# Attention heads of a hybrid SSD/MLA step: maxima turned in the next head's first step, rows moved inside SBUF, more remainders and splits on GpSimd, sample queries prepared for two heads at once

## The chip, the cores and the metric

The kernel runs on one core of one Trainium2 chip. The metric is the device time of the whole program in microseconds (us). Before the change the median of three runs is 2051.01 us (2038.73 to 2052.41). The engines are TensorE (PE, with its weight loads PEld), VectorE (DVE), ScalarE (ACT), GpSimd (POOL) and SyncE (SP), which issues DMAs.

## The reference

Two layers, a Mamba-2 SSD layer and a multi-head latent attention (MLA) layer, on a prompt of 1024 tokens and on eight sample sequences of eight tokens with a paged cache of 2048 positions. The change lies in the MLA layer:

```python
def latent_partial(q_lat, q_pe, ckv, kpe, mask):
    s = (jnp.einsum('bqhc,bkc->bhqk', q_lat, ckv.astype(F32))
         + jnp.einsum('bqhr,bkr->bhqk', q_pe.astype(F32), kpe.astype(F32))) * MLA_SCALE
    if mask is not None:
        s = jnp.where(mask, s, NEG_INF)
    m = jnp.max(s, axis=-1)
    p = jnp.exp(s - m[..., None])
    return m, jnp.sum(p, axis=-1), jnp.einsum('bhqk,bkc->bhqc', p, ckv.astype(F32))

def latent_out(l, acc, w_uv):
    return jnp.einsum('bhqc,chv->bqhv', acc / l[..., None], w_uv.astype(F32))
```

16 heads, 64 + 32 query columns (without and with rotary position) a head, 256 latent columns, 64 value columns. The prompt part is causal; `absorb` multiplies the 64 columns of a query by `w_uk` of its head.

## The kernel before

The program has these stages, one behind the other on PE: the SSD layer (to some 1080 us), the MLA input projections and gates, the queries with the first maxima, the sixteen prompt heads (1384 to 1772 us), and the sample attention with the output projection. float32 precision is kept by splitting each operand into a rounded high part and a low part (`split`: a cast on ACT, a subtraction on the engine named, DVE without a name) and adding three matmuls.

`mla_heads` runs the heads in a loop. A head h has 12 steps: for query half qc = 0 four key blocks jb, for qc = 1 eight. A step is `qk` (three matmuls into a PSUM tile `st`, one mask matmul; ACT makes `th`, the rounded exponential, and `P`, the full one; the remainder `tl` = P - th is a subtraction on one engine), then some "units" of preparation, then `pv` of the step two earlier (`LEAD` = 2; matmuls with th and V high, th and V low, tl and V high). So what a step's remainder is needed for comes two steps later. The last `pv` of a query half is followed by the normalisation: ACT (`rl`), DVE and POOL (`og`), a DMA.

The units are generators that run a piece at a time. `maxpass(h + 1, 0)` and `maxpass(h + 1, 1)` (a and b in the loop) compute the scores of the next head once (`sc`), take their row maxima on DVE (`mx`, `tensor_tensor_reduce` and `reduce_max`), turn them to negative split rows (`nm`), transpose these on PE (`nmp`), copy the result (`nr`) on DVE and write it as rows 96 and 97 of the query tile qTh; `qk` of the next head multiplies 98 rows, so that the maximum is subtracted there. `prep(h + 2)` makes the queries of the head after next (`qT`), its part of the sample queries (`qs`, `ql`, `qpr`), keys (`kp`) for every second head, and, for every fourth head, weights and values of a group of four heads (`prep_group`: `w` splits, `vp`). `merge` interleaves the two lists and each step takes its share of them. Odd heads thus have a short list, heads 4, 8 and 12 one with keys, heads 2, 6 and 10 the longest one.

Order: PE and POOL run their instructions in the order in which the program issues them. For DVE, ACT and SP a scheduler decides ahead of the run; each engine then runs its queue in that order. Scores, transposes and preparation share four PSUM buffers (`wt()`).

Lines that matter below: `sc` L1682, `mx` L1685 and L1687, `nm` L1693 and L1694, `nmp` L1697, `nr` L1699, DMAs L1701 and L1702, `st` L1714 to L1721, `th` and `P` L1725 and L1726, `tl` L1728, `pv` L1745 to L1747, `og` L1757 and L1759, `split` L130 and L131, the generic three-matmul product L89 (of `vp` too), `qs` L1645 and L1647, `ql` L1656, `qpr` L1665 to L1667.

Of the kernel before, what the change touches and what calls it, by code (L numbers as in the profile page):

```python
# [20 lines left out]
NT = 8  # L21
# [1472 lines left out]
class Heads:  # L1494
    def __init__(self, k, st):
        tc, nc, I = k.tc, k.nc, k.I
        self.k, self.psum = k, None
        self.wuk = I["mla_w_uk"][0].rearrange("c h n -> c (h n)")
        self.wuv = I["mla_w_uv"][0].rearrange("c h n -> c (h n)")
        vp = st.enter_context(open_pool(tc, name="vp3", bufs=1))  # L1500
        self.V = []
        self.add_v(vp, 0)
        self.w8 = [vp.tile([128, 2, 256], F32R if i > 1 else F32, name=f"w8{i}") for i in range(8)]
        self.kT = [k.kT]
        self.add_k(vp, 1)
        self.qT = []
        self.add_q(vp, 0)
        self.add_q(vp, 1)

# [58 lines left out]
    def units(self, h):  # L1568
        return 4 + 2 * (h % 2 == 0) + 10 * (h % 4 == 0)

    def prep_group(self, hg):
# [9 lines left out]
        split(k, *self.wk, self.wkr)  # L1581
        split(k, *wv, raw)
# [48 lines left out]
    def prep_q(self, h):  # L1631
# [12 lines left out]
        p = self.wt(f"qs{h}")  # L1644
        nc.tensor.transpose(p[:96, :64], self.qt[:64, 8, 96 * j : 96 * j + 96], k.ident[:64, :64])  # L1645
        for c in range(2):
            nc.tensor.transpose(p[:64, 128 + c * 128 : 256 + c * 128],  # L1647
                                self.wkr[:, c, 64 * (h % 4) : 64 * (h % 4) + 64], k.ident)
        qsn = sp.tile([96, 64], F32, tag="qsn", name=f"qsn{h}", bufs=2)
        nc.vector.tensor_copy(qsn, p[:96, :64])  # L1650
        wt = sp.tile([64, 256], F32, tag="wt", name=f"wt{h}", bufs=2)
        nc.scalar.copy(wt, p[:64, 128:384])
        yield
        pl = self.wt(f"ql{h}p")
        for c in range(2):
            nc.tensor.matmul(pl[:, c * 64 : c * 64 + 64], wt[:, c * 128 : c * 128 + 128], qsn[0:64],  # L1656
                             start=True, stop=True)
        for c in range(2):
            src = pl[:, c * 64 : c * 64 + 64].rearrange("p (b t) -> p b t", t=NT)
            dh = k.qlh[:, c].rearrange("p b (h t) -> p b h t", t=NT)[:, :, h]  # L1660
            dl = k.qll[:, c].rearrange("p b (h t) -> p b h t", t=NT)[:, :, h]
            split(k, dh, dl, src)
        src = qsn[64:96].rearrange("p (b t) -> p b t", t=NT)
        qv = k.qpr.rearrange("p b (h t) -> p b h t", t=NT)[:, :, h]
        nc.vector.tensor_copy(qv[0:32], src)  # L1665
        nc.vector.tensor_copy(qv[32:64], src)
        nc.vector.tensor_tensor(qv[64:96], src, qv[0:32].bitcast(F32), op=ALU.subtract)  # L1667
        yield

    def maxpass(self, h, qc):  # L1670
# [29 lines left out]
        nd = k.dram.tile([2, 512], F32, name=f"nd{h}_{qc}")  # L1700
        nc.sync.dma_start(nd.rearrange("a (i c) -> (a i) c", c=128), nr)  # L1701
        nc.sync.dma_start(qh[96:98, 512 * qc : 512 * qc + 512].bitcast(F32), nd)  # L1702

    def qk(self, h, qc, jb):
# [22 lines left out]
        eng = nc.gpsimd if jb % 2 else nc.vector  # L1727
# [45 lines left out]
def mla_heads(k, hd, sm, early, st):  # L1773
    k.tc.keep_in_program_order(k.nc.scalar.preload_act_table_set("natural_log_exp_and_others"))
    held, late = [], []

    def step(g):
        try:
            next(g)
        except StopIteration:  # L1780
            pass

    for h in range(MH):
# [4 lines left out]
        if h + 1 < MH:  # L1788
            a, b = hd.maxpass(h + 1, 0), hd.maxpass(h + 1, 1)
            units += [a] * 4 + [b, a, b, b, b, a] + [b] * 6  # L1790
# [12 lines left out]
        for t in range(12):  # L1803
            qc, jb = (0, t) if t < 4 else (1, t - 4)
            held.append((h, qc, jb, *hd.qk(h, qc, jb)))
            while done < total * (t + 1) // 12:
                step(units[done])
                done += 1
            if len(held) > LEAD:
                hd.pv(*held.pop(0))  # L1810
# [550 lines left out]
```

## Time and profile before

| | us |
|---|---|
| median of three runs | 2051.01 |
| profiled execution | 2054.24 |
| its span, first to last instruction | 2052.5 |
| mean granted PE clock of the span | 0.968 |
| heads stage, 1384 to 1772 | 388.0 |

In the profile a row of the timeline is start, duration, engine, line, operation, output<-input, and, in brackets, the idle time of the engine just before it and what ended that. In the windows each engine's busy time is followed by its number of instructions; PEclk is the share of the full TensorE clock that was granted. A group of instructions by form gives total busy us, mean ns of one, and idle time before them.

### The profile page before, as it was taken

The numbers are of one execution on the slowest core, as the hardware profiler recorded it, in microseconds if no ns is written. First come the engines' busy times: TensorE is split into PE (matmuls) and PEld (weight loads), VectorE is DVE, ScalarE is ACT, GpSimd is POOL, SyncE is SP. The second block draws the span as 40 slices with busy tenths as digits, with TensorE's granted clock in tenths as the row PEclk, the third lists the DMA queues.
The fourth block names the chain that finished last, engine by engine and source line by source line (L and its number), as shares of the span: only waits on it lengthen the run. The fifth ranks groups of instructions, "written<-read, shape, count | busy, mean of one in ns | idle before, by whom it ended". The sixth has DMA issues, their size and how long they took to land.

```text
span 2052.5 us, 33717 instructions
## 1 busy us (share of the span) xinstructions
PE 1932.4 (94%) x12001; PEld 1765.2 (86%) x12001; DVE 1228.3 (60%) x2652; ACT 1111.3 (54%) x2627; POOL 768.2 (37%) x961
## 2 busy tenths in 40 slices
PE   6989999999999999899999999698999999899998
PEld 5879999999999998677788998697888888778887
DVE  4527675757575666544335134468777778776665
ACT  5446666666666666543325224236666667755552
POOL 1317373636455575331000002004232334755541
PEclk9989999999999999899999999899999999999999
DMA  4113323233332333443546321322111112454451
GB/s 147 41 37 91 91 82 93 87 87 96 89 95 86 90 93 125 163 173 125 182 155 197 144 74 50 102 86 65 44 46 35 49 38 76 150 182 126 148 147 38
DMA packets 186479, 206.56 MB, mean 101 GB/s; under 512 B 23132, under 2 KB 151912, under 8 KB 185928
## 3 DMA queue, kind: packets, MB, share of 16 engines
q1 hardware_dynamic: 181480, 185.40, 29.3%
q0 software_dynamic: 4752, 18.88, 2.8%
q8 instruction: 95, 1.56, 0.3%
q14 instruction: 72, 0.59, 0.1%
q10 hardware_dynamic: 80, 0.13, 0.0%
HBM read 151.05 MB, written 53.28 MB: 100 GB/s over the span
## 4 chain that ended last, share of the span: by engine, by line
PE 71%; DVE 10%; DMA 5%; issue 5%; POOL 4%; ACT 4%; SPq 1%; POOLq 0%; DVEq 0%; ACTq 0%
PE pj L89 21%; PE pj L101 8%; PE pq L101 5%; PE pob L101 4%; PE poa L101 4%; PE py L759 3%; POOL kvl L2009 2%; PE pz L101 1%; PE pk L101 1%; PE p L101 1%; PE sc L1682 1%; PE vp L89 1%; PE st L89 1%; PE st L1714 1%; PE st L1716 1%
## 5 line engine op out<-in xcount | busy, mean ns | idle before, releaser
L89 PE MATMUL pj<-xh,wih 128*128 128x384 f32 (+1 forms) x768 | 254.7, 336 | 8.4 <-ACT xh L236 4.1
L89 PE MATMUL pj<-xl,wih 128*128 128x384 f32 (+1 forms) x768 | 254.1, 331 | 0.0
L89 PE MATMUL pj<-xh,wil 128*128 128x384 f32 (+1 forms) x768 | 252.5, 329 | 0.0
L131 DVE TENSOR_TENSOR wil<-wraw,wih 128x512 fp32r<-128x512 f32 x88 | 70.7, 805 | 160.2 <-ACT wih L130 160.1
L1728 POOL TENSOR_TENSOR tl<-P,th 128x384 fp32r<-128x384 f32 (+1 forms) x96 | 91.3, 952 | 185.6 <-ACT P L1726 142.7
L89 PEld LDWEIGHTS pj<-xh,wih 128*128 128x128 f32 x768 | 145.6, 191 | 10.0 <-ACT xh L236 5.0
L89 PEld LDWEIGHTS pj<-xl,wih 128*128 128x128 f32 x768 | 146.0, 190 | 0.6
L89 PEld LDWEIGHTS pj<-xh,wil 128*128 128x128 f32 x768 | 145.7, 190 | 0.0
L101 PE MATMUL pj<-wih,xh 128*128 128x256 f32 x504 | 143.4, 288 | 0.0
L796 POOL TENSOR_TENSOR y<-y,xD 128x256 f32<-128x256 f32 x64 | 83.9, 1311 | 151.5 <-DVE y L795 141.1
L101 PE MATMUL pj<-wil,xh 128*128 128x256 f32 (+1 forms) x504 | 139.2, 282 | 0.0
L1725 ACT ACTIVATE th<-st 128x512 fp32r<-128x512 f32 x192 | 94.3, 491 | 77.8 <-PE st L1721 59.5
L617 DVE SCALAR_TENSOR_TENSOR acc<-raw,vec,acc 128x1112 f32<-128x1112 f32 x84 | 130.3, 1551 | 0.2
L101 PE MATMUL pj<-wih,xl 128*128 128x256 f32 x448 | 126.6, 283 | 0.0
L131 POOL TENSOR_TENSOR xddl<-xdd,xddh 128x256 fp32r<-128x256 f32 x64 | 64.1, 1001 | 116.7 <-ACT xddh L130 116.7
L2009 POOL TENSOR_TENSOR kvl<-pgr,kvh 128x1024 fp32r<-128x1024 f32 x32 | 78.1, 2439 | 70.1 <-ACT kvh L2008 70.1
L130 ACT CAST Ch<-acc 128x128 fp32r<-128x128 f32 x56 | 16.9, 302 | 155.8 <-PE py L89 155.8
L734 ACT ACTIVATE M<-M,tok 128x128 f32<-128x128 f32 (+1 forms) x288 | 90.5, 388 | 10.4 <-DMA M<-acs_d 10.4
L101 PEld LDWEIGHTS pj<-wih,xh 128*128 128x128 f32 x504 | 96.1, 191 | 0.0
L101 PEld LDWEIGHTS pj<-wil,xh 128*128 128x128 f32 (+1 forms) x504 | 93.1, 185 | 0.6
L1726 ACT ACTIVATE P<-st 128x512 f32<-128x512 f32 x192 | 93.2, 485 | 0.0
L101 PEld LDWEIGHTS pj<-wih,xl 128*128 128x128 f32 x448 | 85.6, 191 | 0.0
(1010 smaller groups left out, 6396.8 us busy)
## 6 DMA issues: line engine op xcount, KB each, us to landing
wraw<-in_ssd_w_in SPq DMA_DIRECT2D x92, 256.0 KB
M<-acs_d SPq DMA_DIRECT2D x64, 256.0 KB
y_d<-xD SPq DMA_DIRECT2D x64, 128.0 KB
s<-in_state_ssm SPq DMA_DIRECT2D x32, 256.0 KB
out_s_ssm<-s SPq DMA_DIRECT2D x32, 256.0 KB
wraw<-in_ssd_w_out SPq DMA_DIRECT2D x16, 512.0 KB
q_d<-qt SPq DMA_DIRECT2D x32, 192.0 KB
qp<-q_d SPq DMA_DIRECT2D x8, 768.0 KB
```

The costliest lines, as they stand in the source:

```text
L89: nc.tensor.matmul(out, a, b, start=(i == 0), stop=(i == n - 1))
L101: nc.tensor.matmul(o, a, b, start=(j == 0), stop=(j == len(ops) - 1))
L131: (eng or nc.vector).tensor_tensor(lo, src, hi.bitcast(F32), op=ALU.subtract)
L617: nc.vector.scalar_tensor_tensor(acc, self.raw[bi][:, j : j + n], k.convw[j][:, blk : blk + 1], acc, op0=ALU.mult, op1=ALU.add)
L734: nc.scalar.activation(M[:m, h, :m], M[:m, h, :m], AF.Relu, bias=c.tk[:, 0, 4 * g + h : 4 * g + h + 1], scale=-1.0)
L759: nc.tensor.matmul(py[:m, h * 64 : h * 64 + 64], c.M[:m, h, :m], c.xdt[:m, h * 64 : h * 64 + 64], start=True, stop=True)
L796: nc.gpsimd.tensor_tensor(y[:m], y[:m], c.xD[:m], op=ALU.add)
L1682: nc.tensor.matmul(ps[:, :n], qh[:96, 128 * i : 128 * i + 128], kh[:96, 512 * c : 512 * c + n], start=True, stop=True)
L1725: nc.scalar.activation(th[:, :n], ps[:, :n], AF.Exp, scale=SCALE)
L1726: nc.scalar.activation(P[:, :n], ps[:, :n], AF.Exp, scale=SCALE)
L1728: eng.tensor_tensor(tl[:, :n], P[:, :n], th[:, :n].bitcast(F32), op=ALU.subtract)
L2009: nc.gpsimd.tensor_tensor(rl, raw, rh.bitcast(F32), op=ALU.subtract)
```

## The change

1. The last step of b (transpose `nmp`, copy `nr`, the row DMAs) leaves the head in which its scores are made. It is carried into the first step of the next head, behind that step's `qk` and units.
2. The copied rows go from `nr` in SBUF directly to the query tile, by two DMAs of 4 x 128 values, instead of one DMA to a buffer in HBM and one back.
3. `tl` is made on POOL for jb = 1, 2, 3, 5, 6, 7 (jb % 4 not 0), 9 of the 12 steps of a head, instead of jb odd, 6 of 12.
4. The subtractions of the weight splits in `prep_group` go from DVE to POOL.
5. The sample queries of two heads are made together, in the odd head's preparation: the two transposed queries stand in a block-diagonal tile `qb` (zeroed once on POOL), so that one 128-column matmul per half does what two did; the rotary part `qpr` is written by POOL. Even heads have two units less.

On PE around the end of a head (the end of head 4; `o` is pv, `st` qk, and the number behind a name is that of its buffer) stood before:

```order
L1682 MATMUL sc_71_17300<-kTh_14729,qTh_15805 128x512
L1745 MATMUL o_1_17211<-th,Vh_15808 128x512
L1746 MATMUL o_1_17211<-th,Vl_15809 128x512
L1747 MATMUL o_1_17211<-tl,Vh_15808 128x512
L1714 MATMUL st_1_7_17309<-qTh_14736,kTh_13521 128x128
L1715 MATMUL st_1_7_17309<-qTl_14737,kTh_13521 128x128
L1716 MATMUL st_1_7_17309<-qTh_14736,kTl_13522 128x128
L1721 MATMUL st_1_7_17309<-mr 128x128
L1656 MATMUL ql6p<-qsn_17279,wt_17281 128x64 x2
L1697 MATMUL nmp_1_17330<-ident,nm_1_17303 8x128
L1745 MATMUL o_1_17211<-th,Vh_15808 128x384
L1746 MATMUL o_1_17211<-th,Vl_15809 128x384
```

In the same place on PE stands now:

```order
L1695 MATMUL sc_71_17252<-kTh_14729,qTh_15790 128x512
L1759 MATMUL o_1_17148<-th,Vh_15793 128x384
L1760 MATMUL o_1_17148<-th,Vl_15794 128x384
L1761 MATMUL o_1_17148<-tl,Vh_15793 128x384
L1728 MATMUL st_0_0_17261<-qTh_15790,kTh_14729 128x512
L1729 MATMUL st_0_0_17261<-qTl_15791,kTh_14729 128x512
L1730 MATMUL st_0_0_17261<-qTh_15790,kTl_14730 128x512
L1735 MATMUL st_0_0_17261<-mr 128x128
L1695 MATMUL sc_00_17273<-kTh_15774,qTh_14733 128x128
L1710 MATMUL nmp_1_17276<-ident,nm_1_17255 8x128
L1759 MATMUL o_1_17148<-th,Vh_15793 128x256
L1760 MATMUL o_1_17148<-th,Vl_15794 128x256
```

The last scores `sc_71` moved a step later, and `nmp` moved behind the first step's qk of the next head; the `ql` matmuls are gone from this even head.

On POOL around the start of a head whose units hold a group's splits (the end of head 5 and the start of head 6; `tl` of 384 columns is the second step's) stood before:

```order
L1728 TENSOR_TENSOR tl<-P,th 128x384
L1728 TENSOR_TENSOR tl<-P,th 128x128
L1728 TENSOR_TENSOR tl<-P,th 128x384
L1759 TENSOR_TENSOR og_17382<-og_17382,rl_1_17383 64x512
L1728 TENSOR_TENSOR tl<-P,th 128x128
L1728 TENSOR_TENSOR tl<-P,th 128x512
L1759 TENSOR_TENSOR og_17472<-og_17472,rl_0_17473 64x512
```

and now:

```order
L1742 TENSOR_TENSOR tl<-P,th 128x384
L1742 TENSOR_TENSOR tl<-P,th 128x256
L1678 CAST qpr<-qsr_17442 32x8x16
L1679 CAST qpr<-qsr_17442 32x8x16
L1680 TENSOR_TENSOR qpr<-qsr_17442,qpr 32x8x16
L1742 TENSOR_TENSOR tl<-P,th 128x128
L1742 TENSOR_TENSOR tl<-P,th 128x384
L131 TENSOR_TENSOR w_14724<-w_14721,w_14723 128x512
L131 TENSOR_TENSOR w_14728<-w_14722,w_14727 128x512
L1773 TENSOR_TENSOR og_17583<-og_17583,rl_1_17584 64x512
L1742 TENSOR_TENSOR tl<-P,th 128x256
L1742 TENSOR_TENSOR tl<-P,th 128x128
```

Between the second step's remainder and `og` two splits came in, the third step's remainder (256 columns) stands behind `og`, and the casts of `qpr` stand before the last remainder of the head ahead.

The diff, cut to its core:

```diff
--- before.py
+++ after.py
@@ -1506,6 +1506,9 @@
         self.qT = []
         self.add_q(vp, 0)
         self.add_q(vp, 1)
+        self.qb = [vp.tile([128, 128], F32, name="qb")]
+        for t in self.qb:
+            nc.gpsimd.memset(t, 0.0)
 
     def start(self, st):
         k, nc = self.k, self.k.nc
@@ -1566,7 +1569,7 @@
         yield from self.prep_q(h)
 
     def units(self, h):
-        return 4 + 2 * (h % 2 == 0) + 10 * (h % 4 == 0)
+        return 4 + 10 * (h % 4 == 0)
 
     def prep_group(self, hg):
         k, nc = self.k, self.k.nc
@@ -1578,8 +1581,8 @@
         raw, wv = w8[1], w8[6:]
         nc.sync.dma_start(raw, self.wuv[:, cs].rearrange("(k p) e -> p k e", p=128))
         yield
-        split(k, *self.wk, self.wkr)
-        split(k, *wv, raw)
+        split(k, *self.wk, self.wkr, nc.gpsimd)
+        split(k, *wv, raw, nc.gpsimd)
         yield
         vh, vl = self.V[hg % 2]
         for i in range(8):
@@ -1641,30 +1644,40 @@
             cs = slice(512 * c, 512 * c + 512)
             split(k, qh[:96, cs], ql[:96, cs], p[:96])
             yield
-        p = self.wt(f"qs{h}")
-        nc.tensor.transpose(p[:96, :64], self.qt[:64, 8, 96 * j : 96 * j + 96], k.ident[:64, :64])
+        if j == 0:
+            return
+        p = self.wt(f"qs{pr}")
+        for jj in range(2):
+            nc.tensor.transpose(p[:96, 64 * jj : 64 * jj + 64], self.qt[:64, 8, 96 * jj : 96 * jj + 96], k.ident[:64, :64])
+        o = (pr % 2) * 128
         for c in range(2):
-            nc.tensor.transpose(p[:64, 128 + c * 128 : 256 + c * 128],
-                                self.wkr[:, c, 64 * (h % 4) : 64 * (h % 4) + 64], k.ident)
-        qsn = sp.tile([96, 64], F32, tag="qsn", name=f"qsn{h}", bufs=2)
-        nc.vector.tensor_copy(qsn, p[:96, :64])
-        wt = sp.tile([64, 256], F32, tag="wt", name=f"wt{h}", bufs=2)
-        nc.scalar.copy(wt, p[:64, 128:384])
+            nc.tensor.transpose(p[:, 128 + c * 128 : 256 + c * 128], self.wkr[:, c, o : o + 128], k.ident)
+        qb = self.qb[0]
+        for jj in range(2):
+            r = slice(64 * jj, 64 * jj + 64)
+            nc.vector.tensor_copy(qb[r, r], p[0:64, r])
+        qr = sp.tile([32, 128], F32, tag="qsr", name=f"qsr{pr}", bufs=1)
+        nc.vector.tensor_copy(qr, p[64:96, :128])
+        wt = sp.tile([128, 256], F32, tag="wt", name=f"wt{pr}", bufs=1)
+        nc.scalar.copy(wt, p[:, 128:384])
         yield
-        pl = self.wt(f"ql{h}p")
+        pl = self.wt(f"ql{pr}p")
         for c in range(2):
-            nc.tensor.matmul(pl[:, c * 64 : c * 64 + 64], wt[:, c * 128 : c * 128 + 128], qsn[0:64],
-                             start=True, stop=True)
+            nc.tensor.matmul(pl[:, c * 128 : c * 128 + 128], wt[:, c * 128 : c * 128 + 128], qb, start=True, stop=True)
+        hs = slice(2 * pr, 2 * pr + 2)
+
+        def pair(t):
+            return t.rearrange("p (j b t) -> p b j t", j=2, t=NT)
+
+        def home(t):
+            return t.rearrange("p b (h t) -> p b h t", t=NT)[:, :, hs]
+
         for c in range(2):
-            src = pl[:, c * 64 : c * 64 + 64].rearrange("p (b t) -> p b t", t=NT)
-            dh = k.qlh[:, c].rearrange("p b (h t) -> p b h t", t=NT)[:, :, h]
-            dl = k.qll[:, c].rearrange("p b (h t) -> p b h t", t=NT)[:, :, h]
-            split(k, dh, dl, src)
-        src = qsn[64:96].rearrange("p (b t) -> p b t", t=NT)
-        qv = k.qpr.rearrange("p b (h t) -> p b h t", t=NT)[:, :, h]
-        nc.vector.tensor_copy(qv[0:32], src)
-        nc.vector.tensor_copy(qv[32:64], src)
-        nc.vector.tensor_tensor(qv[64:96], src, qv[0:32].bitcast(F32), op=ALU.subtract)
+            split(k, home(k.qlh[:, c]), home(k.qll[:, c]), pair(pl[:, c * 128 : c * 128 + 128]))
+        src, qv = pair(qr), home(k.qpr)
+        nc.gpsimd.tensor_copy(qv[0:32], src)
+        nc.gpsimd.tensor_copy(qv[32:64], src)
+        nc.gpsimd.tensor_tensor(qv[64:96], src, qv[0:32].bitcast(F32), op=ALU.subtract)
         yield
 
     def maxpass(self, h, qc):
@@ -1697,9 +1710,10 @@
         nc.tensor.transpose(p[:8, :128], nm.rearrange("p a i -> p (a i)").bitcast(F32), k.ident)
         nr = sp.tile([8, 128], F32, tag="nr", name=f"nr{h}_{qc}", bufs=2)
         nc.vector.tensor_copy(nr, p[:8, :128])
-        nd = k.dram.tile([2, 512], F32, name=f"nd{h}_{qc}")
-        nc.sync.dma_start(nd.rearrange("a (i c) -> (a i) c", c=128), nr)
-        nc.sync.dma_start(qh[96:98, 512 * qc : 512 * qc + 512].bitcast(F32), nd)
+        for a in range(2):
+            row = qh[96 + a : 97 + a, 512 * qc : 512 * qc + 512].bitcast(F32)
+            row = bass.AP(row.tensor, row.offset, [list(row.ap[0]), [128, 4], [1, 128]])
+            nc.sync.dma_start(row, nr[4 * a : 4 * a + 4])
 
     def qk(self, h, qc, jb):
         k, nc, sp = self.k, self.k.nc, self.sp
@@ -1724,7 +1738,7 @@
         P = sp.tile([128, 512], F32, tag="P", name="P", bufs=3)
         nc.scalar.activation(th[:, :n], ps[:, :n], AF.Exp, scale=SCALE)
         nc.scalar.activation(P[:, :n], ps[:, :n], AF.Exp, scale=SCALE)
-        eng = nc.gpsimd if jb % 2 else nc.vector
+        eng = nc.gpsimd if jb % 4 else nc.vector
         eng.tensor_tensor(tl[:, :n], P[:, :n], th[:, :n].bitcast(F32), op=ALU.subtract)
         return th, tl
 
@@ -1772,7 +1786,7 @@
 
 def mla_heads(k, hd, sm, early, st):
     k.tc.keep_in_program_order(k.nc.scalar.preload_act_table_set("natural_log_exp_and_others"))
-    held, late = [], []
+    held, carry = [], None
 
     def step(g):
         try:
@@ -1787,7 +1801,10 @@
             sm.begin(st, hd.psum)
         if h + 1 < MH:
             a, b = hd.maxpass(h + 1, 0), hd.maxpass(h + 1, 1)
-            units += [a] * 4 + [b, a, b, b, b, a] + [b] * 6
+            units += [a] * 4 + [b, a, b, b, b, a] + [b] * 5
+            ready, carry = carry, b
+        else:
+            ready, carry = carry, None
         if h + 2 < MH:
             g = hd.prep(h + 2)
             units = merge(units, [g] * hd.units(h + 2))
@@ -1806,6 +1823,8 @@
             while done < total * (t + 1) // 12:
                 step(units[done])
                 done += 1
+            if t == 0 and ready:
+                step(ready)
             if len(held) > LEAD:
                 hd.pv(*held.pop(0))
     for x in held:
```

## Prediction

> **What bounds the kernel now.** I read the page of the profiled run first, then the windows by stage, the waits of TensorE (PE) in the stage of the sixteen heads, the timeline around one head boundary, and last the groups by form for the price of each operation. The page gives the span and each engine's busy time:
>
> ```profile
> span 2052.5 us, 33717 instructions
> PE 1932.4 (94%) x12001; PEld 1765.2 (86%) x12001; DVE 1228.3 (60%) x2652; ACT 1111.3 (54%) x2627; POOL 768.2 (37%) x961
> ```
>
> PE is busy for 94% of the span, so only time in which PE stands still, or runs at the half clock, or PE work itself, can be won. The edits all lie in the stage of the heads, 1384 to 1772 us. Its windows, with the columns of the first line:
>
> ```profile
> core 0: us, PE busy (x) PEld busy (x) DVE busy (x) ACT busy (x) POOL busy (x), PEclk, DMA share, GB/s
> 1384.00:1772.00 388.00, 364.77 (x1971) 316.12 (x1970) 299.67 (x716) 258.85 (x589) 148.45 (x141) 0.93 0.19 53
> 1500.00:1520.00 20.00, 19.20 (x114) 16.51 (x113) 16.71 (x45) 15.43 (x37) 8.18 (x9) 1.00 0.12 29
> 1520.00:1540.00 20.00, 17.99 (x85) 16.27 (x84) 13.40 (x35) 10.10 (x26) 6.75 (x6) 0.74 0.28 83
> 1600.00:1620.00 20.00, 19.20 (x116) 16.54 (x114) 16.70 (x45) 15.49 (x37) 8.08 (x8) 1.00 0.12 28
> 1620.00:1640.00 20.00, 17.94 (x93) 16.37 (x93) 14.65 (x37) 10.83 (x28) 7.35 (x7) 0.83 0.28 83
> ```
>
> PE idles 388.0 - 364.8 = 23.2 us of this stage. The mean granted clock is 0.93, so 0.07 x 388 = 27 us of full-speed time are not granted either. They come in stretches: 1500 to 1520 has 1.00, the next 20 us 0.74 with fewer matmuls (85 for 114). VectorE (DVE) works 300 of 388 us, GpSimd (POOL) 148. What PE waits for here:
>
> ```profile
> PE nmp L1697 <- DVE nm L1694: 14.0, 11, 2.1
> PE nmp L1697 <- DVE qll L131: 3.2, 4, 0.8
> PE o L1747 <- POOL tl L1728: 0.4, 1, 0.4
> PE o L1747 <- DVE tl L1728: 0.4, 1, 0.4
> ```
>
> 17.2 of the 23.2 us are the transpose nmp, which turns the row maxima of the next head: 15 waits, one at the end of each head but the last. PE takes its instructions in program order, so all of the next head stands behind it. The end of one head in order of time:
>
> ```profile
> 1504.78 0.44 PE L1682 MATMUL sc<-kTh,qTh 96*128 96x512 f32 x1
> ...
> 1505.35 0.76 DVE L1687 CUSTOM_DVE_ANT_0 sc<-sc,mk,mx 128x512 f32<-128x512 f32 x1
> ...
> 1506.25 0.66 PE L1656 MATMUL ql6p<-qsn,wt 64*128 64x64 f32 x4
> ...
> 1506.56 0.42 DVE L1728 TENSOR_TENSOR tl<-P,th 128x256 fp32r<-128x256 f32 x1
> ...
> 1506.88 0.46 POOL L1728 TENSOR_TENSOR tl<-P,th 128x128 fp32r<-128x128 f32 x1 [1.82 <-ACT P L1726]
> 1506.91 0.45 DVE L1693 TENSOR_SCALAR nm<-mx 128x4 fp32r<-128x4 f32 x1
> ...
> 1507.39 0.16 DVE L1694 SCALAR_TENSOR_TENSOR nm<-mx,nm 128x4 fp32r<-128x4 f32 x1
> ...
> 1507.67 0.08 PEld L1697 LDWEIGHTS nmp<-ident,nm 128*8 128x8 f32 x1 [0.91 <-PE ql6p L1656]
> 1507.70 0.27 PE L1697 MATMUL nmp<-ident,nm 128*8 128x128 f32 x1 [0.80 <-DVE qll L131]
> ```
>
> From the last scores (1504.78) to nmp (1507.70) 2.92 us pass. On DVE a remainder of 256 columns stands between the maximum and nm, and nm takes 0.45.
>
> **The change part by part.** *The transpose moves.* Behind the last scores PE will now run three pv matmuls of 384 columns, three of 512, a mask and a narrow score matmul, and only then nmp. Starts of such matmuls in the rows of the next head:
>
> ```profile
> 1513.74 0.34 PE L1747 MATMUL o<-tl,Vh 128*128 128x384 f32 x1
> 1513.91 0.40 PE L1714 MATMUL st<-qTh,kTh 98*128 98x512 f32 x1
> 1514.15 0.40 PE L1715 MATMUL st<-qTl,kTh 98*128 98x512 f32 x1
> ```
>
> 0.17 and 0.24 us apart: 0.24 + 3 x 0.17 + 3 x 0.24, and some 0.1 for the two narrow ones, is 1.6 us from the last scores to nmp. The DVE chain without the remainder and with nm undisturbed is 0.57 to the maximum's start, 0.86 to its end, an estimated 0.17 for nm (about what its second half takes above), and 0.31 from 1507.39 to PE: 1.9 us. Some 0.3 us stay uncovered, 15 times 5 us: the term is -12, between 0 (DVE as late as now) and -17.
>
> *The half clock.* The stretches at the reduced clock begin behind the longer of these waits: in 1500 to 1520 the one wait is the 0.8 above and the clock is full; the row with 0.74 holds this one of 2.0:
>
> ```profile
> 1528.60 0.38 PE L1697 MATMUL nmp<-ident,nm 128*8 128x128 f32 x1 [2.01 <-DVE nm L1694]
> ```
>
>  If such waits shrink, the clock stays up, but new waits (below) can take it down. Of 27 us I take a third, -9, with ends 0 and -20. [...]
>
> *Pairs of sample queries.* The group row of the wide transposes, beside ql6p above:
>
> ```profile
> L1647 PE MATMUL qs<-ident,w 128*64 128x128 f32 x28 | 5.7, 286 | 0.0
> ```
>
> Two heads now use 8 ql matmuls, 2 x 0.66 us; after, 2 wider ones, an estimated 0.4; of six transposes four stay, which spares 2 x 5.7/28 = 0.4 at most. That is about 0.9 us for a pair and seven pairs in this stage: -6, from -3 (latency of a chain counted as work) to -7.
>
> *The rows without the detour through HBM.* Two issues stay two:
>
> ```profile
> 1508.31 0.27 SPq L1701 DMA_DIRECT2D nd<-nr  x1
> 1509.52 0.22 SPq L1702 DMA_DIRECT2D qTh<-nd  x1
> ```
>
> The second now waits for the first to land, 1.2 us from issue to issue. After, both start at once: nr, two issues of 0.27, one landing of up to 1.2. That is some 3 us from nmp. Their reader, the fifth step's qk, stands 4 to 5 us of PE work behind nmp instead of 5.4 to 7.3, because nmp moved towards it. Cost 0 with a spare of about 1 us; if that is gone, see the third rival.
>
> *Remainders and splits to POOL.* Prices by form:
>
> ```profile
> L1728 DVE TENSOR_TENSOR tl<-P,th 128x512 fp32r<-128x512 f32 x64 | 52.4, 818 | 18.0 <-ACT P L1726 17.7
> L1728 POOL TENSOR_TENSOR tl<-P,th 128x512 fp32r<-128x512 f32 x32 | 42.1, 1315 | 44.1 <-ACT P L1726 32.5 <-PE sc L1682 11.0
> L1728 POOL TENSOR_TENSOR tl<-P,th 128x384 fp32r<-128x384 f32 x32 | 34.2, 1069 | 100.5 <-ACT P L1726 82.6 <-PE o L1746 17.8
> L1728 POOL TENSOR_TENSOR tl<-P,th 128x128 fp32r<-128x128 f32 x31 | 14.6, 472 | 38.3 <-ACT P L1726 24.9 <-PE qs L1647 6.7 <-PE nmp L1697 6.4
> L131 DVE TENSOR_TENSOR w<-w,w 128x512 fp32r<-128x512 f32 x5 | 6.5, 1297 | 0.0
> ```
>
> A 256-column remainder on POOL lies between 0.47 and 1.07; I take 0.77. Each head gives POOL one of 512 and two of 256, 1.3 + 2 x 0.77 = 2.9 us, sixteen times 46 us; with six splits of an estimated 1.3 and some 8 for the qpr casts POOL comes to 148 + 62 = 210 of 388 us. In sum it fits; the place is what matters, since POOL is strictly in order. In the head that starts at 1509:
>
> ```profile
> 1511.35 1.02 POOL L1728 TENSOR_TENSOR tl<-P,th 128x384 fp32r<-128x384 f32 x1 [4.02 <-ACT P L1726]
> 1514.32 1.34 POOL L1759 TENSOR_TENSOR og<-og,rl 64x512 f32<-64x512 f32 x1 [1.94 <-PE o L1747]
> 1515.63 0.45 POOL L1728 TENSOR_TENSOR tl<-P,th 128x128 fp32r<-128x128 f32 x1
> ...
> 1515.29 0.28 PE L1747 MATMUL o<-tl,Vh 128*128 128x256 f32 x1
> ```
>
> The third step's remainder (256 columns) is now queued behind og, which ends at 1515.66: it would be ready at 1516.4, and PE asks for it at 1515.29, 1.1 us too early. If DVE, relieved, hands over its part of og sooner, this shrinks. At the seventh step a second og stands in the same way before a remainder of 512. Replaying POOL's queue with the times of before gives 1.1 at the third and 0.55 at the seventh step of the 8 odd heads and 1.3 in three others: 8 x 1.65 + 3.9 = 17 us; 3 if og comes a microsecond sooner. I take +9, the nearer to the row being the upper end, DVE's relief the reason to go below it.
>
> *Splits in the group heads.* In heads 2, 6 and 10 POOL now gets, behind the second step's remainder, two splits, and PE's second vp matmul needs the later one:
>
> ```profile
> 1434.07 0.31 PE L1721 MATMUL st<-mr 128*128 128x128 f32 x1
> ...
> 1435.37 1.00 POOL L1728 TENSOR_TENSOR tl<-P,th 128x384 fp32r<-128x384 f32 x1 [5.43 <-PE o L1746]
> ...
> 1436.21 0.73 PE L89 MATMUL vp<-w,kvh 128*128 128x256 f32 x2
> ```
>
> The remainder ends at 1436.37; two splits of 1.3 end at 1438.97; PE is there at 1436.21 (with the clock halved; a microsecond sooner at the full one). PE waits 2.7 to 3.8 us, three times: +9, from +6 (splits of 0.8, the 512-column row of DVE) to +12. Today DVE makes these splits long before, so nothing of this wait exists. og and the third step's remainder come late behind it, under the same wait.
>
> *The rest.* In the last two heads POOL also makes splits of the gathered cache, and the extra remainders queue with them, each with up to its own 1.3 us: three of them 4, so +2 (0 to 4). The start of the stage and the sample stage keep their order nearly: 0, 3 either way.
>
> **Sum**: -12 - 9 - 6 + 9 + 9 + 2 = -7 us. The profiled execution took 2054.24 us, 1.74 more than its span, and 3.2 more than the median, 2051.01. So 2054.24 - 7 - 3.2 = 2044.
>
> **Rivals.** *First: POOL's lateness is covered.* For it: POOL has 240 us idle here, the relieved DVE brings og forward, and 1 us of lateness is what one matmul group covers. Then nmp's waits and the half clock go: -17 - 20 - 7 + 3 + 6 = -35, 2016 us.
>
> *Second, slower: POOL sets the pace of the pv matmuls.* Place: the remainders behind og and the splits behind the second step's remainder. It decides where a remainder ends on POOL after PE asks for it, which the rows at 1515 already show by 1.1 us. Each such wait takes the place of one at nmp and pulls the clock down again: with +17 for remainders, +12 for splits, +4 at the end, half-clock time up by 7 rather than down, and -5 and -6 for nmp and pairs, +29: 2080 us. Against it: a wait of 0.8 left the clock at 1.00 in the window of 1500.
>
> *Third: the rows come late to the fifth step.* [...] For it: the new transfers are eight pieces of 512 bytes; against it: 1.2 us covered the old one.
>
> *Fourth: the maxima stay as late as they are.* nm took 0.45 beside a POOL remainder of 0.46 that began 0.03 before it, where its second half takes 0.16; a POOL remainder of 512 beside it could hold it 1.3 us, which uses up the ground that nmp gained, and POOL will run more of these. Then nmp keeps its 17 us, the clock wins 4 at most, and POOL's costs come on top: 0 - 4 - 6 + 9 + 9 + 2 = +10, 2061 us. [...]
>
> **How the numbers follow.** About 1% (20.5 us) is what a measurement of this kernel can tell from no change: 2030.5 and 2071.5 are the bounds. Forecast 0.35, first rival 0.33, second 0.18, third 0.07, fourth 0.07. The forecast's own terms reach from -38 to +33; I give 0.02 of it to the faster side. Faster: 0.33 + 0.02 = 0.35; same: 0.33 + 0.07 = 0.40; slower: 0.18 + 0.07 = 0.25. The range takes in the first rival and stops short of the second and third: 2012 to 2075. The forecast's own range, as cases of both signs hold most of the chance, is 2031 to 2064.
>
> **What would show it.** nmp waiting for nm below 6 us in all bears out the first term. PE waiting for POOL's tl by 3 to 17 us, and vp for w by 6 to 12, bear out the costs; if both are near zero, the first rival holds. The clock of the stage tells the second term: 0.95 or more against 0.93. A wait of st for a DMA at the fifth step would be the third rival. What would make me wrong most: a POOL split that runs long before PE asks for it, or waits of 1 us that halve the clock oftener than I took.

## The result and the profile after

The changed kernel takes 2056.99 us (median of 20 runs, 2054.03 to 2059.77), the kernel before 2049.16 us (20 runs, 2038.73 to 2055.07). The ratio is 1.0041, with a 95% interval of 1.003 to 1.0053: the change makes the kernel slower by 0.4%, some 8 us, where a gain of 7 was forecast. The profiled execution of the changed kernel took 2057.51 us, within 1 us of its median; the one of before, 2054.24, lies 5 us above its own.

The page after has less work on PE and DVE, and more on POOL:

```profile
span 2055.7 us, 33651 instructions
...
PE 1917.0 (93%) x11953; PEld 1746.7 (85%) x11953; DVE 1172.9 (57%) x2540; ACT 1108.1 (54%) x2603; POOL 826.8 (40%) x1042
```

PE is busy 15.4 us less (1932.4 before) in a span that is 3.2 us longer: PE stands still for 18.6 us more. The window of the heads stage after, with the columns as in the prediction, and PE's waits in the same window:

```profile
1384.00:1772.00 388.00, 351.38 (x1939) 298.98 (x1938) 250.81 (x619) 256.74 (x570) 204.17 (x216) 0.95 0.20 54
```

```profile
PE o L1761 <- POOL tl L1742: 14.1, 22, 1.1
PE vp L89 <- POOL w L131: 9.6, 3, 3.2
PE o40n L2007 <- ACT pn L2000: 4.4, 1, 4.4
PE nmp L1710 <- DVE nm L1707: 3.5, 6, 0.7
PE o L1761 <- DVE tl L1742: 3.3, 2, 2.8
```

The waits of nmp fell from 17.2 to 3.5 us, as forecast. In their place stand 14.1 us for POOL's remainders (22 waits), 9.6 us for POOL's splits (3 waits), and a wait of 4.4 us in the last head that was 1.2 before. This last one is `o40n`, the first product of the sample attention, whose matmuls already stand between those of head 15; it waits for `pn`, a small copy that ACT makes for it. POOL works 204 us here, close to the 210 that were counted.

Where the time goes by part: the first and the last mask matmul of head 15, after and then before.

```profile
1741.98 0.22 PE L1735 MATMUL st<-mr 128*128 128x128 f32 x1
1771.62 0.27 PE L1735 MATMUL st<-mr 128*128 128x128 f32 x1
```

```profile
1747.83 0.22 PE L1721 MATMUL st<-mr 128*128 128x128 f32 x1
1771.94 0.27 PE L1721 MATMUL st<-mr 128*128 128x128 f32 x1
```

The changed kernel reaches head 15 at 1742.0, 5.8 us ahead, and ends it at 1771.6, 0.3 us ahead: head 15 takes 29.6 us instead of 24.1. What follows takes 2055.7 - 1771.6 = 284.1 us instead of 2052.5 - 1771.9 = 280.6. Against this one execution of before, then, the heads up to 14 did win, and the last head and the sample stage lost it all. Against the second execution of before in the table below, the heads up to 14 do not win: 328.6 us against 325.8. Measured in the same way for every run below, this split (heads 1 to 14; head 15; the rest) carries most of what follows.

### The profile page after: what moved, and what is told of

Read it like the earlier page. It is cut to its first block, busy times and chain, and to the rows that moved or that the text cites. A ratio compares the mean times of both kernels' runs of the same rounds, so it can differ in the third digit from the quotient of the medians.

```text
span 2055.7 us, 33651 instructions
## 1 busy us (share of the span) xinstructions
PE 1917.0 (93%) x11953; PEld 1746.7 (85%) x11953; DVE 1172.9 (57%) x2540; ACT 1108.1 (54%) x2603; POOL 826.8 (40%) x1042
## 4 chain that ended last, share of the span: by engine, by line
PE 70%; DVE 7%; DMA 6%; issue 5%; ACT 5%; POOL 5%; SPq 1%; POOLq 0%; DVEq 0%; ACTq 0%
PE pj L89 21%; PE pj L101 8%; PE pq L101 4%; PE pob L101 4%; PE poa L101 4%; PE py L759 3%; POOL kvl L2028 2%; PE o L1761 1%; PE vp L89 1%; PE pz L101 1%; PE pk L101 1%; DMA tkr<-kpe_dh 1%; PE st L1728 1%; PE p L101 1%; PE st L1729 1%
## 5 line engine op out<-in xcount | busy, mean ns | idle before, releaser
L1742 POOL TENSOR_TENSOR tl<-P,th 128x384 fp32r<-128x384 f32 (+1 forms) x144 | 134.4, 941 | 133.2 <-ACT P L1740 109.7
L130 ACT CAST Ch<-acc 128x128 fp32r<-128x128 f32 x56 | 16.9, 302 | 155.9 <-PE py L89 155.9
L1761 PE MATMUL o<-tl,Vh 128*128 128x512 f32 x192 | 71.4, 372 | 17.4 <-POOL tl L1742 14.1
```

Of the source, the lines that this page charges most:

```text
L1742: eng.tensor_tensor(tl[:, :n], P[:, :n], th[:, :n].bitcast(F32), op=ALU.subtract)
L1761: nc.tensor.matmul(po[:, o:], va, tl[:, :n], start=False, stop=(jb == nj - 1))
```

## The experiments

Each ratio is against the kernel before on the same chip; "heads 1 to 14", "head 15" and "rest" are taken from one profiled execution each, at the mask matmuls as above. Differences between runs are given between medians; reckoned by the ratios they come out up to 3 us otherwise, so a difference of 3 us or less is not told from nothing by the times alone. The parts of one execution differ by chance as well: the same heads 1 to 14 of the changed kernel take 328.6 us here and 326.4, 326.4 and 329.6 in the three runs that edit head 15 only. The windows shown below are all 1402 to 1732 us. This is most of heads 1 to 14; in the faster kernels it reaches into head 15.

| run | median us | ratio, 95% interval | heads 1 to 14 | head 15 | rest |
|---|---|---|---|---|---|
| before (first profile) | 2049.16 | 1 | 336.4 | 24.1 | 280.6 |
| before_again | 2049.06 | 0.9988 [0.9968, 1.0009] | 325.8 | 23.0 | 282.0 |
| the change | 2056.99 | 1.0041 [1.003, 1.0053] | 328.6 | 29.6 | 284.1 |
| splits_on_dve | 2038.43 | 0.9936 [0.9915, 0.9958] | 311.5 | 28.4 | 282.6 |
| remainders_old_rule | 2036.45 | 0.9927 [0.9906, 0.9948] | 313.4 | 23.1 | 282.1 |
| no_pool_moves | 2014.51 | 0.984 [0.9816, 0.9864] | 295.0 | 24.2 | 280.8 |

**The kernel before, a second time** (no edit).

> The kernel before once more, unchanged, for a second profile: its 20 runs spread from 2038.7 to 2055.1 and the profiled one lies at the upper end. Theory (the spread is half-clock time behind the nmp waits, which lie near the length that brings the clock down): a profiled run that is some us faster has fewer half-clock stretches between 1384 and 1772 and the same waits. Rival: the spread comes from another stage (loads from HBM), and the heads stage is equal to 1 us.

The waits of nmp are the same to a tenth of a microsecond, and the clock is not. The windows and the nmp waits in them, the first profile and then the second:

```profile
1402.00:1732.00 330.00, 313.11 (x1704) 272.80 (x1702) 254.03 (x633) 220.39 (x506) 112.50 (x109) 0.92 0.16 46
PE nmp L1697 <- DVE nm L1694: 13.7, 10, 2.1
PE nmp L1697 <- DVE qll L131: 3.2, 4, 0.8
```

```profile
1402.00:1732.00 330.00, 312.04 (x1758) 270.60 (x1756) 262.94 (x653) 227.47 (x520) 119.75 (x116) 0.96 0.19 51
PE nmp L1697 <- DVE nm L1694: 13.7, 10, 2.1
PE nmp L1697 <- DVE qll L131: 3.2, 4, 0.8
```

Both hold 16.9 us of nmp waits (the second has one more wait, of 1.1 us for POOL); 0.92 against 0.96 of the clock is 13 us of full-speed time in 330, and the second execution is 10 us faster, all of it in heads 1 to 14 (325.8 us against 336.4). For this pair the theory holds against the rival: at the same nmp waits the kernel loses 0.04 of its clock more in one execution than in the other. That there is one length near which waits bring the clock down is not shown: in the first profile the waits of 2.04 us that ends at 1431.0 and of 0.85 us that ends at 1461.5 are both followed by a stretch at half the clock, 6.8 and 3.4 us long, and the one of 1.29 us that ends at 1682.3 is not: from 1682 to 1724 the clock is 1.00. The prediction had taken the first execution.

**Splits on DVE again.**

```diff
-        split(k, *self.wk, self.wkr, nc.gpsimd)
-        split(k, *wv, raw, nc.gpsimd)
+        split(k, *self.wk, self.wkr)
+        split(k, *wv, raw)
```

> The changed kernel with the weight splits of a group on DVE again. Theory: the three waits of vp for POOL (9.6 us) and the three half-clock stretches of 6.83 us behind them (10 us of full-speed time) go, heads 2, 6 and 10 shrink from 32.6 to about 27 us, the median falls by 13 to 20 us, to about 2040. Rival (DVE needs the relief): waits of nmp for nm come back at the starts of those heads, 1 to 2 us each with half-clock time, and the median falls by less than 6 us.

2038.43, 18.6 us less than the change. The window and its waits:

```profile
1402.00:1732.00 330.00, 311.11 (x1801) 267.06 (x1801) 230.43 (x578) 236.96 (x525) 173.21 (x187) 1.00 0.19 52
PE o L1761 <- POOL tl L1742: 13.1, 20, 1.1
PE nmp L1710 <- DVE nm L1707: 4.0, 6, 1.0
```

The vp waits are gone, nmp stays at 4 us with the splits on DVE, and the clock is 1.00. So the theory holds and DVE did not need this relief. The row also says something of the second rival: 20 waits of up to 1.1 us for POOL's remainders, and no half clock behind any of them. In the change the same window had three waits of 3.2 us, and 0.97.

**Remainders by the old rule.**

```diff
-        eng = nc.gpsimd if jb % 4 else nc.vector
+        eng = nc.gpsimd if jb % 2 else nc.vector
```

> The changed kernel with the remainders of all heads by the old rule (jb odd on POOL). Theory: the 14.1 us that pv waits for POOL's remainders go, and the nmp waits stay small (under 6 us in all), because the later place of nmp covers DVE's chain without DVE's relief; with the last head's loss gone as well the median falls by 15 to 22 us, to about 2038. Rival (the relief of DVE is what shortened the nmp waits): nmp waits for nm come back to over 10 us, and the median is 2048 or more.

2036.45, 20.5 us less than the change. The window and its waits:

```profile
1402.00:1732.00 330.00, 311.74 (x1786) 271.59 (x1786) 251.69 (x615) 234.76 (x519) 141.19 (x148) 0.96 0.19 51
PE vp L89 <- POOL w L131: 8.9, 3, 3.4
PE nmp L1710 <- DVE nm L1707: 6.7, 6, 1.3
...
PE o L1761 <- POOL tl L1742: 0.6, 1, 0.6
```

POOL's remainders no longer make pv wait; nmp waits 6.7 us, a little over the 6 that the theory gave, far from the rival's 10. Head 15 is back at 23.1 us.

**Both moves to POOL undone**: the two diffs above together; carried transpose, direct rows and pairs stay.

> The changed kernel with both moves to POOL undone: remainders by the old rule and the group's splits on DVE; the carried transpose, the direct rows and the pairs stay. Theory (both moves only cost; their costs add): against the kernel with the old remainder rule (2036.5) the three vp waits (8.9 us) and about 20 us of half clock (10) go as well, the median is 2016 to 2026. Rival (DVE with both loads is too late at the heads' starts): nmp waits come back to over 12 us, the median is 2032 or more.

2014.51, 1.5 us below the expected range. The theory holds: both only cost, and they add. Against this kernel the remainders (splits_on_dve) make heads 1 to 14 longer by 311.47 - 295.03 = 16.4 us and head 15 by 4.2, the splits (remainders_old_rule) heads 1 to 14 by 313.40 - 295.03 = 18.4; the change has 33.6 more there, 5.4 in head 15 and 3.3 behind it. That is 42.3 us, and the medians differ by 42.5. With DVE's remainders and splits as before, its nmp waits are still small:

```profile
1402.00:1732.00 330.00, 320.39 (x1878) 278.88 (x1878) 269.97 (x641) 248.78 (x552) 148.51 (x154) 0.99 0.21 58
PE nmp L1710 <- DVE nm L1707: 4.9, 6, 1.1
```

**The values later, splits on POOL.** This tells the place of a split from its engine.

```diff
     def prep(self, h):
-        yield from self.prep_kv(h)
+        g = self.prep_kv(h)
+        if h and h % 4 == 0:
+            for _ in range(2):
+                next(g)
+                yield
+            yield from self.prep_q(h)
+            yield from g
+            return
+        yield from g
         yield from self.prep_q(h)
```

> The changed kernel, splits still on POOL, but heads 2, 6 and 10 prepare the queries of the head after next before the values: PE comes to the vp matmuls later. Theory (the place in POOL's queue, not the engine's price, makes the three vp waits of 3.2 us, and the half clock is their follower): the vp waits fall from 9.6 us to under 2, the three half-clock stretches go, the median is 2036 to 2044 as with the splits on DVE. Rival (POOL's splits hold up what stands behind them, og and the third step's remainder, whatever PE does): pv waits for POOL instead, in heads 2, 6 and 10, by 2 us or more each, and the median stays over 2048.

2037.66 (0.9952, 0.9934 to 0.997): as much as with the splits on DVE. No wait of vp is left in the window, POOL's remainders are waited for 15.3 us instead of 12.6, and the clock is 0.99:

```profile
1402.00:1732.00 330.00, 310.93 (x1798) 266.92 (x1797) 231.00 (x575) 235.49 (x524) 182.69 (x194) 0.99 0.20 54
PE o L1769 <- POOL tl L1750: 15.3, 23, 1.2
```

The theory holds: the splits cost through the place at which PE asks for them, and not by being on POOL.

**The parts that were meant to win, each alone.** The kernel before with the carried transpose only (parts of the diff of `mla_heads`):

```diff
-            units += [a] * 4 + [b, a, b, b, b, a] + [b] * 6
+            units += [a] * 4 + [b, a, b, b, b, a] + [b] * 5
+            ready, carry = carry, b
...
+            if t == 0 and ready:
+                step(ready)
```

> The kernel before with the carried transpose alone (rows through HBM, queries one head at a time, remainders and splits as before). Theory: the wait of nmp for nm falls from 17.2 to under 8 us without any relief of DVE, and the half-clock stretches of the stage shrink, the median falls from 2050 to 2028 to 2038. Rival (DVE's chain is later than the transpose's new place): nmp waits over 12 us, and the fifth step waits for the rows, which now take two DMAs behind a later start; 2045 or more.

2036.05 (0.9941, 0.9914 to 0.9968): 13 us less than before. DVE's relief is not needed for the nmp waits to go, but the rows through HBM come late in four of the heads, the rival's second half:

```profile
PE st L1714 <- DMA qTh<-nd: 4.6, 4, 2.4
PE nmp L1697 <- DVE nm L1694: 1.8, 4, 0.7
```

The same question in the best kernel, its rows through HBM again (the DMA lines of before put back):

> The kernel with carried transpose, pairs and direct rows (both POOL moves undone), its rows through HBM again. Theory (the carried transpose needs the direct rows, since its rows come 2 to 3 us later: with the transpose alone the fifth step waited 4.6 us for them): waits of st for a DMA of 4 us or more, median 2018 to 2028 against 2014.5. Rival (the rows are hidden either way): no such wait, median 2013 to 2016.

2021.64 (0.9878, 0.9852 to 0.9905), 7.1 us more than no_pool_moves, with 4.1 us of waits of st for the DMA in five steps. The direct rows are worth this, beside a carried transpose.

The kernel before with the pairs of sample queries only (the whole part 5 of the change):

> The kernel before with the sample queries of two heads made together, nothing else. Theory: six us of PE work go (seven pairs of 0.9 us in the heads stage, one before it), and where ql stood between the last scores and nmp its cover goes, so that the nmp waits grow by a few us; net 0 to 6 us below 2050. Rival: the waits take all of it and bring more half clock, 2050 or more.

2021.96 (0.9876, 0.9852 to 0.9899): 27 us where 0 to 6 were expected; neither theory nor rival had it. The nmp waits, with nmp where it was, fell to 9.4 us in 15 waits, none over 1.5, and the clock is whole:

```profile
1402.00:1732.00 330.00, 316.07 (x1847) 273.90 (x1846) 256.69 (x634) 242.59 (x541) 144.57 (x151) 1.00 0.20 55
PE nmp L1710 <- DVE nm L1707: 9.4, 15, 1.5
```

The same with the casts of qpr back on DVE, PE's order unchanged:

```diff
-        nc.gpsimd.tensor_copy(qv[0:32], src)
-        nc.gpsimd.tensor_copy(qv[32:64], src)
-        nc.gpsimd.tensor_tensor(qv[64:96], src, qv[0:32].bitcast(F32), op=ALU.subtract)
+        nc.vector.tensor_copy(qv[0:32], src)
+        nc.vector.tensor_copy(qv[32:64], src)
+        nc.vector.tensor_tensor(qv[64:96], src, qv[0:32].bitcast(F32), op=ALU.subtract)
```

> The kernel with pairs of sample queries alone, its casts of qpr on DVE again; PE's order is the same as with the casts on POOL. Theory (the pairs' 27 us come from PE's work and its order at the end of a head, with DVE's relief a small part): nmp waits 9 to 13 us, the half clock stays away, median 2020 to 2027. Rival (the relief of DVE by the casts is what holds the waits below the length that halves the clock): nmp waits over 14 us, half-clock time over 60 us, median 2035 or more.

2039.96 (0.9961, 0.994 to 0.9981): 18 of the 27 us are gone. The rival holds in the waits (19.0 us, over its 14) and in the time. Its half clock of over 60 us does not show: a clock of 0.98 is some 13 us at half speed in this window.

```profile
1402.00:1732.00 330.00, 308.39 (x1770) 267.21 (x1769) 260.61 (x638) 231.91 (x517) 125.48 (x121) 0.98 0.19 51
PE nmp L1710 <- DVE nm L1707: 19.0, 15, 2.6
```

9.6 us more of waits and 0.02 of the clock in 330 us, 6.6 us, are 16 of the 18. Nearly all of the 9.6 stands at the ends of the seven heads that make the casts, 1.2 to 1.7 us more at each. The timeline shows one group of them:

```profile
1518.44 0.34 DVE L1678 CAST qpr<-qsr 32x128 fp32r<-32x128 f32 x1
1518.79 1.29 POOL L1741 TENSOR_TENSOR tl<-P,th 128x512 fp32r<-128x512 f32 x1
1518.82 1.34 DVE L1679 CAST qpr<-qsr 32x128 fp32r<-32x128 f32 x1
1520.19 0.28 DVE L1680 TENSOR_TENSOR qpr<-qsr,qpr 32x128 fp32r<-32x128 f32 x1
```

The second cast of 32 x 128 takes DVE 1.34 us where POOL has just begun a remainder of 1.29; 1.34 us is also the mean of the seven in the window. The one of the first pair, made at 1349 us, took 0.22. Moved to POOL this cast takes 0.29 to 0.58.

**The last head.** The changed kernel with the old rule for head 15 alone (`jb % (2 if h == MH - 1 else 4)`):

> The changed kernel with one head undone: head 15 makes its remainders by the old rule (jb odd on POOL), all other heads as changed. Theory (the loss sits behind the last head's start: head 15 took 29.6 us against 24.1 before, because extra remainders stand on POOL beside the 2.4 us split of gathered cache rows, a remainder on DVE is held 4.9 us by them, and PE then waits 4.4 us for a copy and runs 10 us at the half clock): the wait of o40n for ACT falls from 4.4 to about 1, head 15 gets 5 us shorter, the median falls from 2057 by 5 to 9 us, to about 2050. Rival (the loss is the sample stage's order alone, or chance of the clock): within 2 us of 2057.

2052.75 (1.0006, 0.9986 to 1.0026): 4.2 us less than the change by the medians, 7 by the ratios, where 5 to 9 were expected; head 15 takes 23.4 us, o40n waits 1.2. The rows of the changed kernel that this undoes, POOL and DVE, then ACT and PE:

```profile
1748.25 1.14 POOL L1742 TENSOR_TENSOR tl<-P,th 128x256 fp32r<-128x256 f32 x2
1749.34 0.60 POOL L1945 CAST tk<-tkr 96x512 fp32r<-96x512 f32 x1
1749.92 2.39 POOL L2028 TENSOR_TENSOR kvl<-pgr,kvh 128x1024 fp32r<-128x1024 f32 x1
1752.28 1.29 POOL L1742 TENSOR_TENSOR tl<-P,th 128x512 fp32r<-128x512 f32 x1
...
1749.22 4.90 DVE L1742 TENSOR_TENSOR tl<-P,th 128x512 fp32r<-128x512 f32 x1 [1.61 <-ACT P L1740]
...
1757.77 0.69 ACT L1971 ACTIVATE P<-sc,nm 128x512 f32<-128x512 f32 x1 [3.68 <-DVE nm L1968]
1759.58 0.24 ACT L2000 COPY pn<-pt40n 8x128 f32<-8x128 f32 x1
1759.87 1.22 PE L2007 MATMUL o40n<-cn,pn 8*128 8x256 f32 x2 [4.39 <-ACT pn L2000]
```

DVE's remainder of 512 columns lasts 4.90 us while POOL works without a gap until 1753.57; nm comes late, and on ACT the small copy pn stands behind the exponential that waits for nm. The scheduler put pn ahead of that exponential before, and again with the old rule in head 15. DVE's remainder, however, stood nearly as long in both: 4.22 us before and 4.20 with the old rule. The rows of before:

```profile
1755.02 4.22 DVE L1728 TENSOR_TENSOR tl<-P,th 128x512 fp32r<-128x512 f32 x1 [1.61 <-ACT P L1726]
1761.49 0.24 ACT L1981 COPY pn<-pt40n 8x128 f32<-8x128 f32 x1
1764.57 0.69 ACT L1952 ACTIVATE P<-sc,nm 128x512 f32<-128x512 f32 x1 [2.84 <-DVE nm L1949]
```

There nm came late too, and cost o40n little (1.2 us), since pn did not stand behind it. So what the change added in head 15 is ACT's order, more than DVE's hold, which grew by 0.7 us only; no run changes the order alone. Two further runs try DVE's remainder alone, by one more `or` in the same line. The first, written with `jb == 4`, moved another key block than the one held:

> The changed kernel with one more remainder on POOL: in head 15 the fifth key block of the second half, the one remainder that DVE held for 4.9 us beside POOL's split of cache rows. [...] Rival (POOL's own lateness is what counts, DVE's long remainder costs nothing): POOL, with 1.3 us more in its queue, makes pv wait longer, and the median is 2057 or above.

2058.21 (1.0054, 1.0032 to 1.0076), where 2050 to 2055 was the author's estimate. The 4.90 us are still there, and so is the wait of 4.4, so it says nothing of what that remainder costs. The second, with `jb == 0`, moves the held one:

> The changed kernel with the remainder of key block 0 of the second half of head 15 on POOL: this is the one that DVE held for 4.9 us (the run last_head_fifth_key_block moved block 4, another one). ACT's order around pn stays as in the changed kernel: pn behind the exponential of the cache scores, which waits for nm from DVE. Theory (two causes in a row: DVE stands while POOL works without a gap, so nm is late, and pn stands behind what waits for nm): nm comes 3 to 4 us sooner, the wait of o40n falls from 4.4 to under 1.5, the median is 2049 to 2055. Rival (DVE waits for POOL or for the scores whatever is taken from it, and only ACT's order counts): o40n still waits 4 us or more, median 2056 or above.

2055.27 (1.0035, 1.0016 to 1.0055), 1.7 us less than the change: in the theory's direction, short of its size (a wait under 1.5, a median to 2055), and too little to tell from nothing by the times. ACT waits 0.96 for nm instead of 3.68, o40n 2.2, head 15 takes 23.8 us. But the next transpose of cache scores, pt, now waits 5.3 us for ACT, and the rest takes 286.9 us instead of 284.1. So within head 15 the loss needs both, pn behind the exponential and a late nm: it goes when either is undone. Most of what this run wins in head 15 is given back in the sample stage.

**A remainder at a better place.** no_pool_moves with one more remainder a head on POOL, key block 6 of the second half, behind no og (`if jb % 2 or jb == 6`):

> The kernel with carried transpose, pairs and direct rows (2014.5), with one more remainder of a head on POOL: key block 6 of the second half, 256 columns, which on DVE stands close ahead of the maxima's end and on POOL behind no og. Theory (what a moved remainder costs is its place: those behind og cost a pv wait of 0.75 to 1.1, this one does not): pv waits for POOL stay under 3 us, the nmp waits fall below 4.9, median 2009 to 2014. Rival (any further POOL work beside DVE's maxima holds up one or the other): pv or nmp waits grow, median 2016 or more.

2013.88, the median of five runs (0.9829, 0.9808 to 0.985), at the upper end of the expected range. nmp waits 3.1 us instead of 4.9, and pv no longer than without this move (1.2 us for DVE and 0.6 for POOL, against 1.3 and 0.7), so a remainder costs nothing that shows at this place; what it wins, 0.6 us between the medians, is too little to tell from nothing. It and no_pool_moves beat both kernels, the one before by 1.6 to 1.7%.

## Why the prediction was wrong, step by step

The step that failed is the price of the moves to POOL, +20 in the sum; they cost 42.5 us. Term by term:

- **The transpose moves, -12**: right. The waits of nmp fell by 13.7 us. The run with this part alone, which relieves DVE of nothing (1.8 us of nmp waits left in the window), shows that the new place did this; the ones with the old remainder rule (6.7) and with both moves undone (4.9) agree.
- **The half clock, -9**: wrong in what it was measured against. The profiled execution of before had 13 us of full-speed time less than its second profile at equal nmp waits. Over the whole stage the clock rose from 0.93 to 0.95, as the prediction asked for; the second profile of before has 0.96 there. And the three vp waits, which the sum counted by their length alone, are each followed by half clock: with the splits on DVE the clock of the window is 1.00, with them on POOL 0.97, 10 us. Around the first of them (1437.3 to 1440.6):

```profile
1420.00:1440.00 20.00, 15.92 (x90) 12.99 (x90) 12.32 (x33) 13.38 (x30) 12.21 (x15) 0.98 0.29 77
1440.00:1460.00 20.00, 19.45 (x105) 17.62 (x106) 9.07 (x23) 10.93 (x25) 8.28 (x9) 0.85 0.15 40
```

  The two rows lack 3.4 us of full-speed time, that is 6.8 us at half the clock, from 1439.2 to 1446.0. The stretches at half the clock last 3.4, 6.8 or 10.2 us in the heads stage of before and 6.8 or 10.2 in that of the change. The length of a wait alone does not decide them: here the clock fell 1.8 us after the wait began, and in the first profile of before three waits of only 0.85 us are each followed by 3.4 us at half the clock (a row of 20 us from 1460 at 0.91), while one of 1.29 us there and 20 of up to 1.1 us in splits_on_dve are followed by none. So the prediction's reading, that the clock falls behind the longer waits alone, was too simple. What decides is not shown here, nor why it differs between executions at equal waits.
- **Pairs, -6**: the sign was right, and a term was missing. Alone they win 27 us, of which 18 by three small DVE operations for each pair that went to POOL; the other 9 were not taken apart. The prediction counted those operations as POOL's load and not as DVE's relief. That DVE stands beside POOL was to be seen before: the 64-column subtraction of `qpr` took 1.2 us in seven heads (1.21 at 1718.33, beside a POOL remainder of 1.34 that began at 1718.11) and 0.22 in the other seven of the stage (at 1506.24, with POOL idle). The pairs share what they win with the carried transpose (13 alone; both and the direct rows together 34.5); this fits in that both act on the same 17 us of waits and their half clock.
- **Direct rows, 0**: right; there is no wait for them in the changed kernel. Their worth shows only against the rows through HBM beside a carried transpose, 7 us.
- **Remainders, +9**: too low, by taking half of its own replay (17) off for DVE's relief. The place was right: in the head that starts at 1509 after, POOL's og ends and the remainder behind it makes pv wait.

```profile
1513.82 1.28 POOL L1773 TENSOR_TENSOR og<-og,rl 64x512 f32<-64x512 f32 x1 [1.31 <-ACT rl L1772]
1515.07 1.13 POOL L1742 TENSOR_TENSOR tl<-P,th 128x256 fp32r<-128x256 f32 x2
...
1515.84 0.38 PE L1761 MATMUL o<-tl,Vh 128*128 128x256 f32 x1 [0.66 <-POOL tl L1742]
```

  It costs 16.4 us in heads 1 to 14, the upper end given (17). DVE's relief brought og forward by half a microsecond, not by a whole one.
- **Splits, +9**: the waits are 9.6 us, as worked out; with their half clock, which the term put at nothing, the cost is 18.4.

```profile
1437.06 1.00 POOL L1742 TENSOR_TENSOR tl<-P,th 128x384 fp32r<-128x384 f32 x1 [2.28 <-PE st L1735]
1438.01 2.49 POOL L131 TENSOR_TENSOR w<-w,w 128x512 fp32r<-128x512 f32 x2
1440.55 0.58 PE L89 MATMUL vp<-w,kvh 128*128 128x256 f32 x1 [3.21 <-POOL w L131]
```

- **The last heads, +2, and the rest, 0**: wrong; 5.4 and 3.3 us. The prediction looked at POOL's queue alone. In head 15 the loss came by way of ACT's order, which put a small copy behind an exponential that waits for DVE, and one of DVE's remainders lasted 4.90 us, until POOL's unbroken row had ended. The cause of the 3.3 us behind it stays open.

The moves to POOL together were put at +20 and cost 42.5; the other parts at -27 and win 34.5. The sign was lost in the first. Of the rivals, the first (POOL's lateness is covered) is refuted by the 14.1 us of waits. The second, slower, has its place right, and is right on the clock for the splits, wrong for the remainders. The third did not happen; where rows came late to five steps (no_pool_rows_hbm), 7.1 us were lost. The fourth did not show at nm, but what it rests on, a DVE operation that lasts as long as the POOL work beside it, showed at the casts (1.34 us beside 1.29) and in head 15 (4.90 us).

## What to carry to other kernels

Work moved to an idle engine is paid where the consumer asks for it: ask, for each operation, what stands ahead of it in the new engine's queue and when its reader comes, and add the clock that is lost with the wait (here 6.8 us at half the clock with each of three waits of 3.2 us). Relief of the old engine was worth something only where it shortened a wait: here three small operations for each pair of heads were worth 18 us ahead of the end of a head, and 56 larger ones elsewhere cost 42. When an operation seems to be the cause because it is slow after the change, see how slow it was before. Try the parts of a change one at a time, and profile the kernel before twice when its runs spread.

## What the runs showed of the hardware

- Two executions of one program (before and before_again), whose waits at nmp were equal to 0.1 us, differed by 0.04 in the mean granted clock over 330 us (0.92 and 0.96), and by 10 us.
- In the heads stage the granted clock of TensorE went to half (0.50 from 1439.2 to 1445.9 in the change) in stretches of 3.4, 6.8 or 10.2 us (before) and of 6.8 or 10.2 us (the change). With each of the three waits of 3.2 us in the changed kernel came one of 6.8, which began 1.8 to 2.1 us after the wait did. In before each of three waits of 0.85 us was followed by one of 3.4, and each of four waits of 0.80 us by none.
- Some VectorE operations lasted as long as what GpSimd was doing beside them: a cast of 32 x 128 took 1.34 us beside a remainder of 1.29 (pairs_casts_on_dve), a subtraction of 32 x 64 took 1.21 us beside a remainder of 1.34 and 0.22 with GpSimd idle (before), and a remainder of 512 columns took 4.90 us beside GpSimd's unbroken row of remainders, cast and split (0.69 at that head's first step; the changed kernel, head 15).
